# Differential attention's output norm: squares moved from GpSimd to ScalarE, their sum and products placed as steps of their own

## The chip, the cores and the metric

One core of one Trainium2 chip runs the whole program. The metric is the device time of one execution in microseconds; what is compared is the median of several runs. TensorE (PE) does matmuls and transposes, VectorE (DVE), ScalarE (ACT) and GpSimd (POOL) the elementwise work, SyncE (SP) issues the DMAs.

## What is computed

Two layers over x (512 tokens by 1024). Each layer normalizes and modulates x, projects it with w_in (1024 by 3712) and feeds three branches whose outputs are concatenated and go through w_out. Branch A is the one that the change touches most:

```python
def diff_attention(q, k, v, lam, lam_init, subln_g):     # 4 heads, two 32-wide softmax maps each, 64-wide values
    ...
    def block(qi):
        s = jnp.einsum('bqhmd,bkhmd->bhmqk', qi, k).astype(jnp.float32) * scale
        p = jax.nn.softmax(s, axis=-1)
        pd = p[:, :, 0] - lam * p[:, :, 1]
        return jnp.einsum('bhqk,bkhd->bqhd', pd.astype(v.dtype), v)
    ...
    return rms_norm(o, subln_g) * (1.0 - lam_init)
```

After it, A's output is multiplied by its own gate (ga). Branch B is dilated attention with gate gb, branch C bidirectional retention, whose output is normalized over 96 columns of each head and gated by gc.

## The kernel before, in words

The projection is cut into **groups**: one group is six matmuls (L338, L339, L340: the weights split into a high and a low part, whi and wlo, times the high and low part of h) for one tile of 128 tokens and two slices of 128 rows of w_in. whi is rounded on ScalarE from the loaded rows, wlo is their difference on VectorE (L307); both live in a pool of three buffers (tags whi and wlo of `wp`), so that a whi can be written only when the matmuls of the third one before it are done. Everything else hangs on this list: `at(g, fn)` plans a step behind group g, and the program is issued group by group with its planned steps. A scheduler then orders the instructions of each engine, moving ahead what it takes to be ready; `tc.keep_in_program_order` ties an instruction to its place behind all that was issued before it on its engine.

Branch A runs as two units per layer, A0 and A1, B as three, B0 to B2, and they overlap: while A0 ends, B0's scores are running, and while A1 ends, B1's and B2's and branch C's gate. A unit of A (class `Diff`) does its scores (L724), the maximum mx (L726), exp into e on ScalarE, the mix of two maps on VectorE, four transposes through the one transposing PSUM buffer (`tr4`, L555), copies pt, and the pv product (L701). `finish` copies pv to oat; `finish2`, four groups later, transposes oat, copies it to oao (ScalarE), squares it on GpSimd into oasq (L748), sums the squares on VectorE (L752), multiplies twice by r0 (L753, L754) and ends the norm with `rms_end` (L570 on VectorE, a power of -1/2 on GpSimd, L198). `finish3` multiplies by r0 once more (L761), scales oao (L762) and multiplies by ga on GpSimd (L764); `finish4` transposes and splits the result. B's units have scores L785 and L786, a custom maximum L790, a softmax kept in sb (ScalarE) with its reciprocal L796. The scores of A and B, and ada_ps (the sums for the modulation), share two PSUM buffers (`sc_p`). "nat" is q and k after transposing (two writes by ScalarE, two by VectorE, which must be done before the transposing buffer is free), "qkn" their normalized form. Branch C squares its output on ScalarE already (csq), sums on VectorE (css, L962), and multiplies (L968) C_NORM groups after its product; its gate is cth (tanh on ScalarE from the projection's PSUM, then L158 on VectorE), whose buffers the first matmuls of gb (L334) wait for. The gate of the layer's output (ScalarE, gate<-ada_ps) lives in two buffers that ga uses too, so it waits for L764.

Of the kernel before, what the change touches and what calls it, by code (L numbers as in the profile page):

```python
# [9 lines left out]
F32 = mybir.dt.float32  # L10
F32R = mybir.dt.float32r
AF = mybir.ActivationFunctionType
OP = mybir.AluOpType
AX = mybir.AxisListType
# [5 lines left out]
P = 128  # L20
# [20 lines left out]
MODS = 12  # L41
H_0, H_1 = 8, 9
C_GAP, C_DECAY, C_TURN, C_STATE = 3, 4, 4, 7
C_ATT, C_PAIR, C_OUT, C_STEP, C_SUMS, C_NORM = 8, 3, 13, 2, 1, 7
GATE, GATE_GAP, GATE_END = 55, 24, 18
GB_OUT = 9
SETUP, TABLES, RET_T, TAB1 = 12, 12, 19, 9      
N_A1, N_B1, N_SOFT = 5, 5, 9
E_T1, E_T2, E_X, E_QF, E_SCALE_A, E_SCALE_B = 1, 1, 1, 0, 0, 0
FIN2, FIN3, FIN4 = 4, 12, 16  # L50
X_BACK = 2


# [80 lines left out]
def encoder(ctx, tc, x, c, norm_g, w_ada, b_ada, w_in, w_out, params, consts, out):  # L134
# [9 lines left out]
    sm = pool("sm", 4)  # L144
# [6 lines left out]
    V, A, G, T = nc.vector, nc.scalar, nc.gpsimd, nc.tensor  # L151
    dma = nc.sync.dma_start

    def act(o, i, f=AF.Copy, **kw):
        A.activation(o, i, f, **kw)  # L155
# [7 lines left out]
    def at(g, fn, *args):  # L163
        plan.setdefault(g, []).append((fn, args))
# [180 lines left out]
    def tok_(t):  # L345
        return slice(t * P, (t + 1) * P)
# [205 lines left out]
    def tr4(blocks):  # L552
        ps = tr_p.tile([P, 4, P], F32, name="tr")
        for i, b in enumerate(blocks):
            T.transpose(ps[:, i, :], b, ident)  # L555
        return ps
# [12 lines left out]
    def rms_end(s, n, width):  # L569
        V.tensor_scalar(s, s, 1.0 / width, EPS, OP.mult, OP.add)  # L570
        pow_half(s, s, n)
# [132 lines left out]
    class Diff(Attention):  # L704
# [38 lines left out]
        def finish2(self, g):  # L743
            ps = tr4([self.ob[:, tok_(t)] for t in range(NT)])
            o = self.o = ep.tile([P, 8, DV_A], F32, name="oao", tag="e")
            act(o.rearrange("p g d -> p (g d)"), ps.rearrange("p t m -> p (t m)"))
            sq = ep.tile([P, 8, DV_A], F32, name="oasq", tag="e")
            G.tensor_tensor(sq, o, o, OP.mult)  # L748
            ss = self.ss = sm.tile([P, 8], F32, name="oass")
            r0 = self.r0 = sm.tile([P, 8], F32, name="oar0")  # L750
            V.reciprocal(r0.rearrange("p (t h) -> p t h", h=2), self.ssum[:, :, 0::2])
            V.tensor_reduce(ss, sq, AX.X, OP.add)  # L752
            V.tensor_tensor(ss, ss, r0, OP.mult)  # L753
            V.tensor_tensor(ss, ss, r0, OP.mult)  # L754
            rms_end(ss, 8, DV_A)
            at(g + FIN3, self.finish3)
            at(g + FIN4, self.finish4)

        def finish3(self):
            o, ss = self.o, self.ss  # L760
            V.tensor_tensor(ss, ss, self.r0, OP.mult)  # L761
            V.tensor_tensor(o, o, ss.unsqueeze(2).to_broadcast([P, 8, DV_A]), OP.mult)  # L762
            on = o.rearrange("p (t h) d -> p t (h d)", h=2)
            G.tensor_tensor(on, on, self.u.ga, OP.mult)  # L764
# [65 lines left out]
    class Retention:  # L830
# [129 lines left out]
        def sums(self, n):  # L960
            ss = self.ss[n] = sm.tile([P, H_C], F32, name="css")
            tc.keep_in_program_order(V.tensor_reduce(ss, self.sq[n], AX.X, OP.add))  # L962
            rms_end(ss, H_C, DV_C)
# [335 lines left out]
```

## Time and profile before

| | |
|---|---|
| median of 3 runs | 650.28 us (649.83 to 650.92) |
| the profiled execution's own time | 653.0 us |
| its span | 651.2 us, mean granted TensorE clock 0.989 |
| PE, DVE, ACT, POOL busy | 625.5, 496.8, 340.2, 164.4 us |

The rows further down are times from the start of that span. A row of the timeline that has brackets tells how long its engine stood idle in front of it and what ended that. Idle time of TensorE is the only idle time that lengthens this program directly, and a time saved elsewhere counts when it shortens one of those.

### The profile page before, as it was taken

Reading aid. Unit: us, or ns where it says so; the run is one execution under the profiler, and the core shown is the slowest. Engines: PE = TensorE matmul, PEld = TensorE weight load, DVE = VectorE, ACT = ScalarE, POOL = GpSimd, SP = SyncE. Lnnn points to the kernel's source line nnn. Section 1 sums busy time; section 2 is a strip of 40 time slices with the busy share of each in tenths; the row PEclk is TensorE's granted clock in tenths of the full one; section 3 lists DMA queues with packets and bytes.
Section 4 is the critical chain, followed back from the end, with each engine's and each line's share of the span. In section 5 each row is a group of like instructions: output and inputs, shape, how many; then the busy total and the mean of one; then the engine's idle time right before and its main releaser. Section 6 shows DMA issues by size and latency. Waiting matters only on the chain.

```text
span 651.2 us, 10473 instructions
## 1 busy us (share of the span) xinstructions
PE 625.5 (96%) x3487; PEld 514.2 (79%) x3487; DVE 496.8 (76%) x1212; ACT 340.2 (52%) x750; POOL 164.4 (25%) x183
## 2 busy tenths in 40 slices
PE   6999999999999996999999999999999999899997
PEld 1878888987888873677779998997788787677786
DVE  1889776789978986997869374778997996677543
ACT  4744362666746665564434244455756567656410
POOL 1105462514360510200411041632323340010000
PEclk9799999999999998999999999999999999999999
DMA  9987123426565557476643322235555453603211
GB/s 315 334 290 207 40 82 88 133 91 152 147 177 167 125 172 175 141 254 224 185 169 96 90 72 67 77 101 154 142 171 137 142 142 103 163 32 139 89 64 65
DMA packets 87133, 93.03 MB, mean 143 GB/s; under 512 B 7044, under 2 KB 68132, under 8 KB 87080
## 3 DMA queue, kind: packets, MB, share of 16 engines
q1 hardware_dynamic: 87080, 92.37, 47.8%
q8 instruction: 28, 0.46, 0.3%
q14 instruction: 25, 0.20, 0.1%
HBM read 72.42 MB, written 4.19 MB: 118 GB/s over the span
## 4 chain that ended last, share of the span: by engine, by line
PE 77%; DVE 11%; issue 5%; POOL 3%; DMA 2%; ACT 2%; SPq 0%; POOLq 0%; ACTq 0%; DVEq 0%
PE acc L338 15%; PE acc L340 15%; PE acc L339 15%; PE tr L555 8%; PE pv L701 5%; PE sc L724 2%; PE acc L334 2%; PE acc L335 1%; PE acc L336 1%; DVE ada_acc L158 1%; PE sc L785 1%; DVE wlo L307 1%; PE sc L786 1%; PE line L519 1%; PE co L954 1%
## 5 line engine op out<-in xcount | busy, mean ns | idle before, releaser
L338 PE MATMUL acc<-whi,hT 128*128 128x384 f32 (+1 forms) x424 | 155.1, 366 | 0.0
L339 PE MATMUL acc<-wlo,hT 128*128 128x384 f32 (+1 forms) x424 | 152.3, 359 | 0.0
L340 PE MATMUL acc<-whi,hL 128*128 128x384 f32 (+1 forms) x424 | 152.0, 358 | 0.0
L307 DVE TENSOR_TENSOR wlo<-raw,whi 128x384 fp32r<-128x384 f32 (+1 forms) x130 | 81.8, 658 | 27.0 <-ACT whi L155 26.7
L198 POOL TENSOR_TENSOR qkss<-qkss,nhalf 128x4 f32<-128x4 f32 (+1 forms) x40 | 52.6, 1316 | 128.3 <-DVE qkss L570 125.7
L338 PEld LDWEIGHTS acc<-whi,hT 128*128 128x128 f32 x424 | 79.9, 188 | 6.1
L340 PEld LDWEIGHTS acc<-whi,hL 128*128 128x128 f32 x424 | 79.8, 188 | 6.2
L339 PEld LDWEIGHTS acc<-wlo,hT 128*128 128x128 f32 x424 | 79.9, 188 | 5.5
L155 ACT ACTIVATE whi<-raw 128x768 fp32r<-128x768 f32 (+2 forms) x67 | 59.6, 890 | 36.8 <-PE acc L340 34.0
L158 DVE SCALAR_TENSOR_TENSOR ada_acc<-raw,cs,ada_acc 128x512 f32<-128x512 f32 x86 | 64.4, 750 | 7.1 <-DMA raw<-in_w_ada_dram 5.9
L155 ACT ACTIVATE e<-sc,mx 128x512 f32<-128x512 f32 x64 | 43.9, 688 | 35.8 <-DVE mx L726 17.2
L726 DVE TENSOR_REDUCE mx<-sc 128x1 f32<-128x512 f32 x64 | 43.5, 685 | 9.6 <-PE sc L724 9.1
L155 ACT ACTIVATE sb<-sb,mx 128x512 f32<-128x512 f32 x48 | 34.4, 717 | 20.5 <-DVE mx L790 20.2
L701 PE MATMUL pv<-pt,v 128*64 128x256 f32 x320 | 40.1, 394 | 0.6 <-DVE pt L691 0.5
L155 ACT ACTIVATE pt<-tr 128x512 f32<-128x512 f32 x40 | 23.8, 596 | 24.2 <-PE tr L555 24.1
L790 DVE CUSTOM_DVE_ANT_0 sb<-sc,cst 128x512 f32<-128x512 f32 x48 | 32.1, 684 | 5.4 <-PE sc L786 3.5
L555 PE MATMUL tr<-cst,sb 128*128 128x128 f32 x192 | 30.5, 282 | 5.3 <-DVE nat L158 2.2
L701 PEld LDWEIGHTS pv<-pt,v 128*64 128x64 f32 x320 | 21.7, 140 | 16.6 <-DVE pt L691 5.3
L555 PEld LDWEIGHTS tr<-cst,sb 128*128 128x128 f32 x192 | 22.1, 142 | 15.8 <-ACT pt L155 7.3
L691 DVE COPY pt<-tr 128x512 f32<-128x512 f32 x40 | 27.4, 684 | 8.4 <-PE tr L555 8.4
L622 POOL TENSOR_TENSOR qkn<-qkraw,qkss 128x256 f32<-128x256 f32 x40 | 30.4, 760 | 5.8 <-DVE qkraw L618 2.0
L724 PE MATMUL sc<-stk,stq 96*128 96x512 f32 x64 | 27.3, 434 | 0.9 <-ACT e L155 0.9
(293 smaller groups left out, 1368.9 us busy)
## 6 DMA issues: line engine op xcount, KB each, us to landing
raw<-in_w_ada_dram SPq DMA_DIRECT2D x64, 256.0 KB, 4.8
raw<-in_w_in_dram SPq DMA_DIRECT2D x48, 192.0 KB, 2.6
raw<-in_w_in_dram SPq DMA_DIRECT2D x24, 384.0 KB, 3.9
raw<-in_w_in_dram SPq DMA_DIRECT2D x32, 256.0 KB, 3.6
raw<-in_w_ada_dram SPq DMA_DIRECT2D x16, 512.0 KB, 5.4
raw<-in_w_out_dram SPq DMA_DIRECT2D x32, 256.0 KB, 2.8
x<-in_x_dram SPq DMA_DIRECT2D x8, 512.0 KB, 3.5
stB<-nat SPq DMA_DIRECT2D x32, 128.0 KB, 2.3
```

The source lines that it names most:

```text
L155: A.activation(o, i, f, **kw)
L158: V.scalar_tensor_tensor(o, a, s, b, op0, op1)
L198: G.tensor_tensor(o, i, nhalf[:, :n], OP.pow)
L307: V.tensor_tensor(l2[:, z], r2[:, z], h2[:, z].bitcast(F32), OP.subtract)
L338: T.matmul(ps, ah, hi[i], start=s_, stop=False)
L339: T.matmul(ps, ah, lo[i], start=False, stop=False)
L340: T.matmul(ps, al, hi[i], start=False, stop=e_)
L555: T.transpose(ps[:, i, :], b, ident)
L701: T.matmul(self.pv[h * 64:h * 64 + 64, i * 256:i * 256 + 256], self.u.v[:, k, h * 64:h * 64 + 64], self.pt[h][:, k], start=k == 0, stop=k ...
L724: T.matmul(ps, self.u.stq[0:96, m, tok_(qt)], self.u.stk[0:96, m], start=True, stop=True)
L726: V.tensor_reduce(mx, ps, AX.X, OP.max, negate=True)
L790: V.tensor_tensor_reduce(sb, ps, cst[:, m0:m0 + S], 1.0, 3e38, OP.add, OP.min, mx)
```

## The change

The squares go to ScalarE. Their sum, the two products by r0 and `rms_end` become a step `sums` that is planned FIN_S = 2 groups behind `finish2`, with the sum tied to its place; the third product is tied to its place at FIN3 = 12 groups behind. For branch C, sum and product are each planned one group later.

```diff
-C_ATT, C_PAIR, C_OUT, C_STEP, C_SUMS, C_NORM = 8, 3, 13, 2, 1, 7
+C_ATT, C_PAIR, C_OUT, C_STEP, C_SUMS, C_NORM = 8, 3, 13, 2, 2, 8
...
-FIN2, FIN3, FIN4 = 4, 12, 16
+FIN2, FIN_S, FIN3, FIN4 = 4, 2, 12, 16
...
             sq = ep.tile([P, 8, DV_A], F32, name="oasq", tag="e")
-            G.tensor_tensor(sq, o, o, OP.mult)
-            ss = self.ss = sm.tile([P, 8], F32, name="oass")
+            act(sq, o, AF.Square)
             r0 = self.r0 = sm.tile([P, 8], F32, name="oar0")
             V.reciprocal(r0.rearrange("p (t h) -> p t h", h=2), self.ssum[:, :, 0::2])
-            V.tensor_reduce(ss, sq, AX.X, OP.add)
+            at(g + FIN_S, self.sums, sq)
+            at(g + FIN3, self.finish3)
+            at(g + FIN4, self.finish4)
+
+        def sums(self, sq):
+            r0 = self.r0
+            ss = self.ss = sm.tile([P, 8], F32, name="oass")
+            tc.keep_in_program_order(V.tensor_reduce(ss, sq, AX.X, OP.add))
             V.tensor_tensor(ss, ss, r0, OP.mult)
             V.tensor_tensor(ss, ss, r0, OP.mult)
             rms_end(ss, 8, DV_A)
-            at(g + FIN3, self.finish3)
-            at(g + FIN4, self.finish4)
 
         def finish3(self):
             o, ss = self.o, self.ss
-            V.tensor_tensor(ss, ss, self.r0, OP.mult)
+
+            tc.keep_in_program_order(V.tensor_tensor(ss, ss, self.r0, OP.mult))
```

In the changed program the sum is L758, the two products L759 and L760, the third L766, the scaling of oao L767; B's scores L785 and L786 become L790 and L791, and other lines behind it move by five too.

The order of VectorE at the end of A0 in layer 0, as a difference (plus: changed program; names with numbers are one of several buffers; rt, qkraw and qkss belong to the next unit's q and k):

```order
-L691 COPY pt<-tr 128x4x128
-L616 TENSOR_TENSOR rt_2330<-qkraw,ropebs 128x64
-L617 TENSOR_TENSOR rt_2329<-qkraw,ropebc 128x64
-L761 TENSOR_TENSOR oass<-oass,oar_2138 128x8
-L762 TENSOR_TENSOR oao<-oao,oass 128x512
-L307 TENSOR_TENSOR wlo<-raw,whi 128x384 x2
-L608 TENSOR_REDUCE qkss<-qkn 128x4
-L726 TENSOR_REDUCE mx<-sc 128x1
-L570 TENSOR_SCALAR qkss<-qkss 128x4
+L570 TENSOR_SCALAR qkss<-qkss 128x4
+L307 TENSOR_TENSOR wlo<-raw,whi 128x384 x2
+L608 TENSOR_REDUCE qkss<-qkn 128x4
```

The third product L761 and the scaling L762 go from this place (their successors L766 and L767 come some 60 rows further down), so that nothing that waits for GpSimd's power stands in front of the maximum mx. The sum, L758 for L752, stays where it was, eight rows above this piece, and waits for ScalarE in place of GpSimd.

The order of ScalarE in layer 1 where A1 ends, as a difference (nat_6346 and nat_6348 are the two halves that ScalarE writes):

```order
 L155 ACTIVATE nat_6346<-tr,gcol 128x256
-L155 ACTIVATE sb,bs<-sb,mx 128x512
+L155 ACTIVATE sb<-sb,bs 128x512
+L155 ACTIVATE whi<-raw 128x2x384
 L155 ACTIVATE nat_6348<-tr,gcol 128x256
-L155 ACTIVATE sb<-sb,bs 128x512
-L155 ACTIVATE pt<-tr 128x4x128
-L155 ACTIVATE whi<-raw 128x2x384
+L155 ACTIVATE pt<-tr 128x4x128
 L155 ACTIVATE sb,bs<-sb,mx 128x512 x2
```

The rounding of a weight, whi, stood behind both halves of nat and behind a copy pt; now it stands, with a row sb, between the two halves. A few rows further down, at all four ends of a unit, oasq stands right behind oao or one row later, ahead of the e, cth and pt that follow.

TensorE in layer 1 at the same place, first the program before (the rows behind the last B scores up to the next ones):

```order
L338 MATMUL acc<-whi,hT 128x384
L339 MATMUL acc<-wlo,hT 128x384
L340 MATMUL acc<-whi,hL 128x384
L338 MATMUL acc<-whi,hT 128x384
L339 MATMUL acc<-wlo,hT 128x384
L340 MATMUL acc<-whi,hL 128x384
L338 MATMUL acc<-whi,hT 128x384
L555 MATMUL tr<-cst,sb 128x128 x4
L339 MATMUL acc<-wlo,hT 128x384
L340 MATMUL acc<-whi,hL 128x384
L555 MATMUL tr<-cst,sb 128x128 x4
```

and the changed one, from the transposes of qkn on:

```order
L555 MATMUL tr<-cst,qkn 128x128 x4
L338 MATMUL acc<-whi,hT 128x384
L790 MATMUL sc<-stB,stC 128x512
L791 MATMUL sc<-stB,stC 128x512
L339 MATMUL acc<-wlo,hT 128x384
L340 MATMUL acc<-whi,hL 128x384
L338 MATMUL acc<-whi,hT 128x384
L339 MATMUL acc<-wlo,hT 128x384
L340 MATMUL acc<-whi,hL 128x384
L555 MATMUL tr<-cst,sb 128x128 x8
L790 MATMUL sc<-stB,stC 128x512
L791 MATMUL sc<-stB,stC 128x512
```

Between the transposes of qkn and the next of sb there were twelve matmuls of groups, and there are six; of the two matmuls between two fours of transposes of sb none is left, since the groups run further ahead of this chain. The whi of the piece above goes into the buffer whose last readers are these matmuls: it can start when the sixth is done. In layer 0 the same chain loses three matmuls between two such fours. The step gate<-ada_ps moves too: in layer 0 by six rows of ScalarE, in layer 1 by seventeen, behind three roundings of weights and two copies pt, because the ga product in front of it (L764, on GpSimd) comes later.

## Rows read from the trace of the kernel before

**Rows 1.** From the page's parts 1 and 4: busy time and share of the span of each engine with its number of instructions, and the shares of the chain that ended last.

```profile
PE 625.5 (96%) x3487; PEld 514.2 (79%) x3487; DVE 496.8 (76%) x1212; ACT 340.2 (52%) x750; POOL 164.4 (25%) x183
...
PE 77%; DVE 11%; issue 5%; POOL 3%; DMA 2%; ACT 2%; SPq 0%; POOLq 0%; ACTq 0%; DVEq 0%
```

**Rows 2.** Timeline of layer 0, around the end of branch A's first unit, 184 to 211 us, of ScalarE, VectorE and TensorE. Columns: start, duration, engine, line, operation, out<-in, count, and in brackets the idle time before and what ended it.

```profile
184.76 0.60 ACT L155 ACTIVATE pt<-tr 128x512 f32<-128x512 f32 x1
...
185.44 0.62 PE L555 MATMUL tr<-cst,sb 128*128 128x128 f32 x4
...
186.58 0.69 DVE L752 TENSOR_REDUCE oass<-oasq 128x8 f32<-128x512 f32 x1 [1.90 <-POOL oasq L748]
...
189.94 0.17 DVE L761 TENSOR_TENSOR oass<-oass,oar 128x8 f32<-128x8 f32 x1 [0.89 <-POOL oass L198]
...
193.11 0.68 DVE L726 TENSOR_REDUCE mx<-sc 128x1 f32<-128x512 f32 x1
...
194.71 0.50 PE L785 MATMUL sc<-stB,stC 128*128 128x512 f32 x1 [0.94 <-ACT e L155]
...
210.23 0.50 PE L724 MATMUL sc<-stk,stq 96*128 96x512 f32 x1 [0.87 <-ACT e L155]
```

**Rows 3.** The same view at the same place of layer 1, 494 to 509 us.

```profile
494.92 0.21 DVE L616 TENSOR_TENSOR rt<-qkraw,ropebs 128x64 f32<-128x64 f32 x1
...
497.39 0.74 DVE L616 TENSOR_TENSOR rt<-qkraw,ropebs 128x64 f32<-128x64 f32 x1
...
497.01 1.04 POOL L748 TENSOR_TENSOR oasq<-oao 128x512 f32<-128x512 f32 x1
...
498.74 0.61 ACT L155 ACTIVATE pt<-tr 128x512 f32<-128x512 f32 x1
...
499.41 0.65 PE L555 MATMUL tr<-cst,sb 128*128 128x128 f32 x4
...
501.22 0.17 DVE L761 TENSOR_TENSOR oass<-oass,oar 128x8 f32<-128x8 f32 x1 [1.75 <-POOL oass L198]
...
508.25 0.50 PE L785 MATMUL sc<-stB,stC 128*128 128x512 f32 x1 [0.56 <-ACT e L155]
```

**Rows 4.** Timeline of TensorE in layer 1 around the end of A's second unit, 556 to 570 us: transposes, the pv product and gb's first matmul; the column in brackets is its idle time and who ended it.

```profile
556.23 0.60 PE L555 MATMUL tr<-cst,qkn 128*128 128x128 f32 x4
556.59 0.42 PE L339 MATMUL acc<-wlo,hT 128*128 128x384 f32 x1
...
557.30 0.34 PE L340 MATMUL acc<-whi,hL 128*128 128x384 f32 x1
557.48 0.34 PE L338 MATMUL acc<-whi,hT 128*128 128x384 f32 x1
...
559.30 0.63 PE L555 MATMUL tr<-cst,sb 128*128 128x128 f32 x4
...
560.62 0.66 PE L555 MATMUL tr<-cst,sb 128*128 128x128 f32 x4 [0.34 <-ACT pt L155]
...
562.06 1.95 PE L701 MATMUL pv<-pt,v 128*64 128x256 f32 x16 [0.31 <-DVE pt L691]
...
569.03 0.79 PE L334 MATMUL acc<-hT,whi 128*128 128x512 f32 x1 [0.32 <-DVE cth L158]
```

**Rows 5.** The same stretch, ScalarE and VectorE.

```profile
556.87 0.48 ACT L155 ACTIVATE nat<-tr,gcol 128x256 fp32r<-128x256 f32 x1 [1.53 <-PE tr L555]
...
557.95 0.46 ACT L155 ACTIVATE nat<-tr,gcol 128x256 fp32r<-128x256 f32 x1
...
560.46 0.83 ACT L155 ACTIVATE whi<-raw 128x768 fp32r<-128x768 f32 x1
...
558.68 0.48 DVE L158 SCALAR_TENSOR_TENSOR nat<-tr,gcol,nat 128x256 fp32r<-128x256 f32 x1
...
567.41 0.60 ACT L155 ACTIVATE oao<-tr 128x512 f32<-128x512 f32 x1 [2.19 <-PE tr L555]
567.91 0.48 ACT L155 ACTIVATE cth<-acc 128x384 f32<-128x384 f32 x1
...
576.70 0.60 ACT L155 ACTIVATE gate<-ada_ps 128x512 f32<-128x512 f32 x1
```

**Rows 6.** The same place of layer 0: TensorE's idle times, the pv product, and ScalarE's and TensorE's rows around the gate, 249 to 273 us.

```profile
249.53 0.63 PE L555 MATMUL tr<-cst,sb 128*128 128x128 f32 x4 [2.23 <-DVE nat L158]
...
252.37 3.12 PE L701 MATMUL pv<-pt,v 128*64 128x256 f32 x16
...
271.45 0.60 ACT L155 ACTIVATE gate<-ada_ps 128x512 f32<-128x512 f32 x1 [1.50 <-POOL oao L764]
...
272.10 0.50 PE L785 MATMUL sc<-stk,stq 128*128 128x512 f32 x1 [0.63 <-ACT gate L155]
```

**Rows 7.** Granted clock of TensorE by stretch (the windows view: PE, weight load, DVE, ACT and POOL busy with counts, clock, DMA share, GB/s).

```profile
250.00:260.00 10.00, 7.61 (x42) 4.36 (x40) 5.17 (x13) 4.42 (x9) 0.43 (x1) 0.83 0.83 199
570.00:580.00 10.00, 10.00 (x52) 7.58 (x52) 7.72 (x22) 5.45 (x12) 3.16 (x2) 0.89 0.00 0
```

**Rows 8.** Tile view of branch C's squares: each operation with its minimum, median and maximum in ns; below, who waited for it.

```profile
L155 ACT ACTIVATE csq<-cno x8: 513/525/526, 110.7 to 431.0; 128x384 f32<-128x384 f32 x8
  DVE css L962: 10.2, 6
```

## What the change does to the time, predicted before it ran

> **What bounds the kernel now.** I read the page first, then TensorE's timeline from end to end for every place where it stands idle, then the other engines' timelines at those places. TensorE is busy for 625.5 of 651.2 us [rows 1], so the whole program has 25.7 us in which it waits, and a change that leaves its work alone can move the time only through that remainder. The chain that ended last agrees: 77% TensorE, 11% VectorE, 2% ScalarE, 3% GpSimd [rows 1]. GpSimd's squares, which the change takes away, are therefore worth nothing by their own duration; the question is which TensorE waits lie behind them, and which new ones come.
>
> Two kinds of places matter. Where a unit A0 ends, groups of projection matmuls are plentiful and TensorE hardly waits: 0.94 us at 194.71 and 0.87 us at 210.23 in layer 0 [rows 2], 0.56 us at 508.25 in layer 1 [rows 3]. Where A1 ends, the groups have run out, and TensorE follows a chain of transposes, copies on ScalarE and VectorE, and further transposes: 2.23 us before one transpose in layer 0 [rows 6], 0.34, 0.31 and 0.32 us before three instructions in layer 1 [rows 4]. There each half microsecond that a link of the chain gains or loses goes straight into the time, and each group matmul that was already spent is missing as cover.
>
> **The change part by part.**
>
> *Squares off GpSimd, A0.* VectorE's sum waited 1.90 us for GpSimd's squares and the third product 0.89 us for its power; the score maximum behind them began at 193.11, and the exp, hence TensorE's scores, came late by 0.94 us [rows 2]. In layer 1 the product alone waited 1.75 us, and TensorE 0.56 us after it [rows 3]. In the changed order the third product is no longer in front of that maximum, and the sum waits for ScalarE. Both TensorE waits are shorter than the VectorE waits in front of them, so I count both as gone: 0.94 + 0.56 = 1.50 us. The 0.87 us at 210.23 stand after a copy and an exp on ScalarE that the change does not touch: counted as unchanged, 0.87 us for the low end.
>
> *Squares on ScalarE.* No row has this instruction. Branch C's squares of 384 columns take 0.525 us [rows 8]; a ScalarE copy of 512 columns takes 0.60 us and the next one starts 0.50 us after it (567.41 to 567.91) [rows 5]. So what stands behind is put back by 0.40 us (the squares, less the 0.10 us of overlap) to 0.60 us; I take 0.50, the row of the same width. At A0 that falls on pt: it was ready 0.08 us before its transposes began in layer 0 (184.76 + 0.60 against 185.44) [rows 2] and 0.06 us in layer 1 (498.74 + 0.61 against 499.41) [rows 3], so TensorE would wait 0.42 and 0.44 us, if no more matmuls come between; the change has them in other places, so I take 0 and 0.86 us as bounds and 0.34 us for both together, nearer to the middle since one more matmul (0.18 us, 557.30 to 557.48 [rows 4]) covers part.
>
> *cth behind the squares, A1.* At both ends of A1 the squares stand between oao and cth. gb's first matmul already waited 0.32 us for cth in layer 1 [rows 4], so nothing covers the shift: 0.50 us each, 1.00 us. Bounds 0.80 and 1.20 us by those of the instruction.
>
> *Groups that ran ahead, A1.* In layer 0 three matmuls are missing between transposes, 0.53 us. In layer 1 two are missing where TensorE waits 0.34 us for pt already [rows 4], 0.35 us. Together 0.88 us; the low bound is 0, where the chain itself comes that much earlier.
>
> *The rounding whi between the halves of nat, layer 1.* This is the largest term. Count from the start of the qkn transposes (556.23) [rows 4]. The first half of nat starts 0.64 us later (556.87) [rows 5]. The six matmuls that are left, and the two score matmuls, are through at about 1.95 us, and the last one's end, 2.11 us, is what whi waits for. ScalarE runs whi for 0.83 us and overlaps the next by 0.10 us [rows 5], so the second half of nat starts at about 2.85 us where it started at 1.72 (557.95) [rows 5]. From there to the next transposes the trace has 1.35 us (557.95 to 559.30) [rows 4, 5], of which 0.27 us are a VectorE row in front of its half (558.41 to 558.68). The transposes thus start between 3.93 and 4.20 us, and TensorE has been idle since 1.95: 1.98 to 2.25 us of new wait. The single transposing buffer lets nothing pass. I take 1.90 us, since the clock of these rows can differ by a little; the low bound is 0, if whi's buffer comes free before or the chain runs ahead.
>
> *Moved for nothing.* The gate in layer 0 cost TensorE 0.63 us, because it waited 1.50 us for GpSimd's ga product with a score buffer held [rows 6]. It now stands further down; that 0.63 us goes, but the two score pairs behind it share one PSUM buffer and each waits for VectorE's reading (0.68 us for a row of that width [rows 2]). I set these against each other: 0, with −0.63 and +0.8 us as bounds. In layer 1 the gate was at 576.70 without a wait of TensorE [rows 5]; its delay is the same risk, +0.8 us. Branch C's sum waited 10.2 us for its squares [rows 8], all on VectorE while TensorE had groups; one group later takes these waits away and shortens nothing. SP and its DMAs change places by single rows; loads are far ahead.
>
> Here GpSimd's share of the memory interfaces is to be weighed. While its squares run (497.01 to 498.05), a VectorE product with two inputs takes 0.74 us, where the same one takes 0.21 us else [rows 3]. So one of the four squares cost VectorE 0.53 us. The Trainium skill (GPSIMD Engine Reference, section Key points) says that GpSimd shares its SBUF interfaces with VectorE and contends with VectorE instructions of two SBUF inputs; the trace agrees at this place. By that rule the sum would have up to 0.53 us less, if VectorE were what TensorE waits for there. The row's place is the one whose TensorE wait is counted as gone already, so I add nothing.
>
> **The sum**: −1.50 + 0.34 + 1.00 + 0.88 + 1.90 = +2.62 us. It is made against the profiled execution (653.0 us, span 651.2); the median of the three runs is 650.28, 2.7 us below, and the difference is put on the median: 652.9 us.
>
> **The rivals.** What a measurement tells from no change is about 0.2%, 1.3 us: faster is below 649.0, slower above 651.6.
>
> *Faster.* The order of the chain at A1 is written for a TensorE that is later than it will be, and VectorE sets the pace. If the 2.79 and 1.75 us that VectorE no longer waits bring the chain forward, the waits of 0.94, 0.87, 0.56 and 0.63 us all go (3.0 us), the group matmuls that ran ahead were covered, and only the two cth cost 1.00 us: 648.3 us. For it: all four lie behind GpSimd or VectorE. Against: at the end of A1 TensorE's waits name pt and cth, and GpSimd stands behind none of them [rows 4]. It decides if the second half of nat in layer 1 is ready before the six matmuls are done.
>
> *No change.* All terms hold but the wait behind whi, because whi's buffer is free earlier or ScalarE takes nat's second half in time: +2.62 − 1.90 = +0.72, 651.0 us. For it: 0.72 is what is left of many small terms of both signs.
>
> *Slower by more.* TensorE's granted clock was 0.83 of full in the ten us after the 2.23 us wait of layer 0, and 0.89 from 570 us in layer 1 [rows 7]; the pv product of sixteen matmuls took 3.12 us in the first [rows 6] and 1.95 in the second [rows 4], so half the clock costs it 1.17 us. If the new wait in layer 1 puts pv at the lower level too, and the gate's buffer costs 0.8 us, it is 652.9 + 1.17 + 0.8 = 654.9 us.
>
> **How the numbers follow.** Forecast (slower by the wait behind whi) 0.42; slower by more 0.11; no change 0.25; faster 0.22. The likeliest is the forecast, 652.9 us; its own range, from 0.7 less of the whi wait and of the chain to 0.8 more for the gate, is 651.6 to 654.0. Signs of both kinds hold weight, so the range reaches to the faster case and past the slower: 648.1 to 655.1 us.
>
> **What would show it.** Right: in the changed trace ScalarE's cth starts about 1.0 us after oao in place of 0.5, at both ends of A1; the scores at the two A0 places start without 0.94 and 0.56 us; in layer 1 the transposes of sb behind those of qkn stand 1.5 to 2.3 us behind nat; the gate of layer 1 starts ten us or more after 576.70. Wrong: no wait above 0.5 us at those transposes (then 651.0 or less), or TensorE's idle total below 23 us in place of 25.7 (then faster); a longer stretch below full clock with the same waits would be the slower rival.

## The result, and the profile after

The changed kernel takes 656.06 us (median of 20 runs, 651.3 to 658.03), the kernel before 651.92 us on the same chip (20 runs, 649.08 to 655.4). The ratio is 1.0058, 95% interval 1.0040 to 1.0076: slower by 3.8 us (the two medians lie 4.1 us apart). The forecast's sum was +2.62 us, a ratio of 1.0040; the time itself lies 1 us above the range, for two reasons of unequal kind: the loss is 1.2 us larger than the sum, and the three runs that the sum was put on (650.28 us) lie 1.6 us below the twenty. Three executions far above all others (694.59 us of e1, 2127.04 us of e11, 3431.2 us of the kernel before, beside e5 to e8) are left out of every ratio.

The profiled execution of the changed kernel took 656.07 us. From its page, the parts shown of before in [rows 1]: span, busy time, chain that ended last.

```profile
span 654.3 us, 10490 instructions
...
PE 627.6 (96%) x3487; PEld 516.9 (79%) x3487; DVE 491.1 (75%) x1212; ACT 341.8 (52%) x754; POOL 157.4 (24%) x179
...
PE 89%; DVE 7%; ACT 2%; issue 1%; DMA 1%; SPq 0%; POOL 0%; DVEq 0%
```

The span grew by 3.1 us (651.2 to 654.3). TensorE does the same 3487 instructions and is busy 2.1 us longer, with a granted clock whose mean fell from 0.989 to 0.984. Its idle time grew by only 1.0 us, but that is a balance: 4.1 us of its waits are gone, and 5.5 us are new or longer. Gone are 0.94, 0.87 and 0.63 us in layer 0 [rows 2, 6] and 0.56 us in layer 1 [rows 3], and two more that the prediction did not name (0.57 us in front of transposes at 162 us, 0.54 us in front of a matmul at 322 us). New, or longer, are these. TensorE's timeline in both layers, idle time in brackets:

```profile
261.12 0.79 PE L334 MATMUL acc<-hT,whi 128*128 128x512 f32 x1 [0.97 <-DVE cth L158]
...
537.03 1.95 PE L701 MATMUL pv<-pt,v 128*64 128x256 f32 x16 [1.18 <-DVE pt L691]
...
557.48 0.60 PE L555 MATMUL tr<-cst,qkn 128*128 128x128 f32 x4
...
559.31 0.34 PE L340 MATMUL acc<-whi,hL 128*128 128x384 f32 x1
...
561.67 0.63 PE L555 MATMUL tr<-cst,sb 128*128 128x128 f32 x4 [2.02 <-DVE nat L158]
...
562.98 0.65 PE L555 MATMUL tr<-cst,sb 128*128 128x128 f32 x4 [0.69 <-ACT pt L155]
...
572.06 0.80 PE L334 MATMUL acc<-hT,whi 128*128 128x512 f32 x1 [0.97 <-DVE cth L158]
```

ScalarE in layer 1, the counterpart of [rows 5]:

```profile
558.74 0.45 ACT L155 ACTIVATE nat<-tr,gcol 128x256 fp32r<-128x256 f32 x1
559.10 0.71 ACT L155 ACTIVATE sb<-sb,bs 128x512 f32<-128x512 f32 x1
559.71 0.82 ACT L155 ACTIVATE whi<-raw 128x768 fp32r<-128x768 f32 x1
560.44 0.46 ACT L155 ACTIVATE nat<-tr,gcol 128x256 fp32r<-128x256 f32 x1
...
569.78 0.60 ACT L155 ACTIVATE oao<-tr 128x512 f32<-128x512 f32 x1 [2.19 <-PE tr L555]
570.41 0.63 ACT L155 ACTIVATE oasq<-oao 128x512 f32<-128x512 f32 x1
570.95 0.85 ACT L155 ACTIVATE cth<-acc 128x384 f32<-128x384 f32 x2
...
593.00 0.60 ACT L155 ACTIVATE gate<-ada_ps 128x512 f32<-128x512 f32 x1 [0.81 <-POOL oao L769]
```

Both chains of the forecast can be followed. whi stands between the halves of nat; the second half starts at 560.44, 1.70 us after the first, and TensorE, whose last group matmul began at 559.31, waits 2.02 us. The squares stand between oao and cth: cth starts 1.17 us after oao where it was 0.50, and gb's first matmul waits 0.97 us where it was 0.32 us [rows 4].

The 1.18 us at 537.03 are a new place. VectorE and GpSimd in front of it, same timeline:

```profile
533.91 1.27 DVE L570 TENSOR_SCALAR qkss<-qkss 128x4 f32<-128x4 f32 x1
...
536.30 0.68 DVE L691 COPY pt<-tr 128x512 f32<-128x512 f32 x1
...
533.87 1.28 POOL L769 TENSOR_TENSOR oao<-oao,ga 128x512 f32<-128x512 f32 x1
```

A VectorE operation on four columns takes 1.27 us where its median is 0.16 us, and it ends (535.18) within 0.03 us of GpSimd's ga product (535.15), which the later third product has brought beside it. The copy pt, which pv waits for, stands a few operations behind it on VectorE. The place is new, but the effect is not: the trace of before has it on the same line of code in layer 0.

```profile
219.28 0.61 DVE L570 TENSOR_SCALAR qkss<-qkss 128x4 f32<-128x4 f32 x1
...
220.54 0.16 DVE L570 TENSOR_SCALAR qkss<-qkss 128x4 f32<-128x4 f32 x1
...
219.25 0.61 POOL L622 TENSOR_TENSOR qkn<-qkraw,qkss 128x256 f32<-128x256 f32 x1
219.82 1.06 POOL L198 TENSOR_TENSOR qkss<-qkss,nhalf 128x4 f32<-128x4 f32 x1
```

Beside GpSimd's product of 256 columns (L622) the operation takes 0.61 us and ends with it; beside GpSimd's power of four columns (L198) it takes 0.16 us. The Trainium skill (GPSIMD Engine Reference, section Key points) says that GpSimd shares its SBUF interfaces with VectorE, and that there is contention with VectorE instructions that have two SBUF inputs or run in a 2-port performance mode. This operation has one input; whether it runs in such a mode no run here shows.

The granted clock, in the windows view (PE, weight load, DVE, ACT, POOL busy with counts, clock, DMA share, GB/s):

```profile
40.00:60.00 20.00, 18.39 (x92) 15.82 (x91) 16.95 (x41) 7.68 (x13) 10.10 (x20) 0.83 0.87 244
...
260.00:275.00 15.00, 14.03 (x69) 10.32 (x68) 12.49 (x33) 7.70 (x18) 2.16 (x2) 0.89 0.41 133
555.00:580.00 25.00, 19.31 (x111) 13.70 (x110) 13.87 (x37) 12.95 (x27) 1.64 (x1) 0.93 0.40 106
```

and the second of these windows in before:

```profile
260.00:275.00 15.00, 13.97 (x73) 9.86 (x72) 14.02 (x35) 8.08 (x18) 4.34 (x4) 1.00 0.46 160
```

After the 0.97 us at 261.12 the stretch to 275 us has 0.89, where before has 1.00; from 555 us both have 0.93. The stretch from 40 us, far from any edit, has 0.83. Two more profiles of the same changed kernel (e4 and e10) have 0.89 again from 260 us, but 1.00 from 40 us and 0.86 from 555 us: some of the stretches that fall to the lower level (1.2 GHz in place of 2.4) differ from one execution of a kernel to the next. So one profile cannot price the clock, and the experiments below compare means over runs.

### The profile page after: what moved, and what is told of

It reads as the page before. It is cut to its first block, busy times and chain, and to the rows that moved or that the text cites. A ratio compares the mean times of both kernels' runs of the same rounds, so it can differ in the third digit from the quotient of the medians.

```text
span 654.3 us, 10490 instructions
## 1 busy us (share of the span) xinstructions
PE 627.6 (96%) x3487; PEld 516.9 (79%) x3487; DVE 491.1 (75%) x1212; ACT 341.8 (52%) x754; POOL 157.4 (24%) x179
## 3 DMA queue, kind: packets, MB, share of 16 engines
HBM read 72.42 MB, written 4.19 MB: 117 GB/s over the span
## 4 chain that ended last, share of the span: by engine, by line
PE 89%; DVE 7%; ACT 2%; issue 1%; DMA 1%; SPq 0%; POOL 0%; DVEq 0%
PE acc L340 18%; PE acc L338 18%; PE acc L339 17%; PE tr L555 10%; PE pv L701 6%; PE sc L724 3%; PE acc L334 2%; PE acc L335 2%; PE acc L336 2%; PE sc L790 2%; PE sc L791 2%; PE line L519 1%; PE co L959 1%; DVE ada_acc L158 1%; PE kv L926 1%; PE co L958 1%
## 5 line engine op out<-in xcount | busy, mean ns | idle before, releaser
L307 DVE TENSOR_TENSOR wlo<-raw,whi 128x384 fp32r<-128x384 f32 (+1 forms) x130 | 78.6, 634 | 35.0 <-ACT whi L155 34.7
L198 POOL TENSOR_TENSOR qkss<-qkss,nhalf 128x4 f32<-128x4 f32 (+1 forms) x40 | 55.7, 1393 | 133.6 <-DVE qkss L570 93.8
L622 POOL TENSOR_TENSOR qkn<-qkraw,qkss 128x256 f32<-128x256 f32 x40 | 28.5, 712 | 7.7 <-DVE qkraw L618 2.0
```

The costliest lines, as they stand in the source:

```text
L198: G.tensor_tensor(o, i, nhalf[:, :n], OP.pow)
L307: V.tensor_tensor(l2[:, z], r2[:, z], h2[:, z].bitcast(F32), OP.subtract)
```

## The experiments

**Theories.** T1, that of the forecast: TensorE's waits set the time, made of cth behind the squares, the wait behind whi, and the waits at A0. T2: the waits are only a part, and the granted clock that goes with them is most of the loss. T3, which came up later: what makes the neighbourhood fragile is that cth is taken from the ring of five buffers (tag "e" of `ep`) that oao, oasq, oat, sb and e share; with a buffer of its own gb's matmuls need not stand behind that chain.

Two columns below are worked out from the runs. "Waits" is the sum of TensorE's waits of 0.05 us or more in the profiled execution (before 21.67, change 22.85 us). One of these waits, for the constants' load at the start, lies between 4.16 and 5.22 us without any edit that touches it (before 4.17, change 4.26, e1 5.22, e2 4.75, e3 4.16, e4 4.89, e6 4.55 us), so differences of less than 1 us in this column need it taken off. "Full clock" is an estimate: over all runs together, time fits a constant of the kernel plus some 533 us times (1 − mean granted clock) within 0.6 us rms, and the constant is the time that the kernel would have at clock 1.0. Ratios are to the kernel before on the same chip, with 95% intervals. e1 to e4 share a chip, and so do e5 to e8, e9 to e12 and e13 to e15; from one of these groups to another the ratios are the safer comparison. e1 to e8 have twelve runs each, e9 and e12 four, e11 and e13 to e15 six.

| run | median us | ratio | waits us | mean clock | full clock us |
|---|---|---|---|---|---|
| before | 651.92 | 1 | 21.67 | 0.990 to 0.991 | 647.05 |
| the change | 656.06 | 1.0058 (1.0040 to 1.0076) | 22.85 | 0.984 | 647.15 |
| e1 C only | 653.76 | 1.0010 (0.9988 to 1.0032) | 22.03 | 0.987 | 646.4 |
| e2 A only | 655.27 | 1.0039 (1.0020 to 1.0058) | 21.22 | 0.983 | 646.0 |
| e3 A only, squares late | 650.54 | 0.9976 (0.9955 to 0.9996) | 20.19 | 0.989 | 644.7 |
| e4 the change again | 656.94 | 1.0049 (1.0023 to 1.0075) | 23.42 | 0.983 | 647.2 |
| e5 the change, squares late | 653.35 | 1.0022 (1.0002 to 1.0042) | 21.97 | 0.987 | 646.3 |
| e6 engine of the squares only | 655.13 | 1.0041 (1.0024 to 1.0057) | 22.11 | 0.984 | 646.1 |
| e7 A only, A1's squares on GpSimd | 652.56 | 1.0013 (0.9993 to 1.0034) | 21.02 | 0.988 | 645.9 |
| e8 as e3, without the ties | 650.61 | 0.9969 (0.9950 to 0.9988) | 20.46 | 0.990 | 644.65 |
| e9 before, cth's own buffer | 638.71 | 0.9808 (0.9786 to 0.9830) | 13.62 | 0.996 | 636.9 |
| e11 the change, cth's own buffer | 633.88 | 0.9730 (0.9710 to 0.9750) | 11.39 | 0.997 | 632.4 |
| e12 as e8, cth's own buffer | 639.16 | 0.9804 (0.9781 to 0.9828) | 13.87 | 0.996 | 636.2 |
| e13 A only, cth's own buffer | 638.18 | 0.9788 (0.9762 to 0.9815) | 12.37 | 0.995 | 635.1 |
| e14 C only, cth's own buffer | 637.24 | 0.9776 (0.9752 to 0.9801) | 12.59 | 0.996 | 635.1 |
| e15 as e6, cth's own buffer | 639.12 | 0.9801 (0.9775 to 0.9827) | 12.88 | 0.996 | 636.4 |

**e1, C's part alone.** Only the table line of the diff.

```diff
-C_ATT, C_PAIR, C_OUT, C_STEP, C_SUMS, C_NORM = 8, 3, 13, 2, 1, 7
+C_ATT, C_PAIR, C_OUT, C_STEP, C_SUMS, C_NORM = 8, 3, 13, 2, 2, 8
```

> Branch C's sum and product one group later, branch A as before. Theory (the new TensorE wait comes from the order around whi): in this order too the rounding whi stands between the two halves of nat in layer 1, so TensorE waits 2.0 us before the transposes of sb there and 0.69 in place of 0.34 before the next ones; A0's waits of 0.94, 0.87 and 0.56 us remain, cth waits stay at 0.31 and 0.32. TensorE's idle total 24 us in place of 21.7; time +2.4 us (ratio 1.004), up to +3.6 if the clock drops there too. Rival (C's step is hidden, the wait comes from A's part): idle total 21.7, ratio 1.000.

TensorE's timeline of this kernel in layer 1:

```profile
558.02 0.33 PE L340 MATMUL acc<-whi,hL 128*128 128x384 f32 x1
...
560.36 0.63 PE L555 MATMUL tr<-cst,sb 128*128 128x128 f32 x4 [2.01 <-DVE nat L158]
```

The wait behind whi comes with C's one-group delay by itself, without any edit of branch A. Against the expectation, 0.94 and 0.87 us of layer 0's A0 are gone in it too, and the time does not change measurably (+0.1%, interval across 1). So the largest term of the sum belonged to the part that the prediction had listed under "moved for nothing".

**e2, A's part alone**: the diff without that line.

```diff
-C_ATT, C_PAIR, C_OUT, C_STEP, C_SUMS, C_NORM = 8, 3, 13, 2, 2, 8
+C_ATT, C_PAIR, C_OUT, C_STEP, C_SUMS, C_NORM = 8, 3, 13, 2, 1, 7
```

> Branch A's change alone, C's constants as before. Theory: no whi between the halves of nat, so no 2.02 us wait; A0's waits of 0.94, 0.87 and 0.56 us and the gate's 0.63 are gone, cth waits 0.97 twice; idle total 19.5 to 21 us, time 0.5 to 2 us below before (ratio 0.997 to 0.999) and 2.5 to 4 us below the whole change. Rival (squares on ScalarE cost what the change costs): ratio 1.004 or more, idle total above 22.

No wait of 2.0 us, as expected; yet 1.0039 where 0.997 to 0.999 was expected. Its waits are 0.45 us less than before's (1.03 us less without the wait at the start), but its clock is as low as that of the whole change. The 0.87 us of A0 are still there, so it is C's line that removes them, and gb waits 0.97 us for cth in layer 0 and 0.52 us in layer 1. VectorE and TensorE of this kernel:

```profile
533.46 0.69 DVE L691 COPY pt<-tr 128x512 f32<-128x512 f32 x1
534.06 1.16 DVE L570 TENSOR_SCALAR qkss<-qkss 128x4 f32<-128x4 f32 x1
...
261.25 0.52 PE L334 MATMUL acc<-hT,whi 128*128 128x512 f32 x1 [0.97 <-DVE cth L158]
```

Here VectorE's small operation is stretched beside the ga product too (1.16 us), but stands behind the copy pt, and no pv waits. The 1.18 us of the whole change thus take both parts: A's moves the product there, C's puts the copy behind the operation.

**e3, A's part with the squares two groups later**, behind cth instead of ahead of it; **e5**, the same in the whole change.

```diff
         def finish2(self, g):
...
-            sq = ep.tile([P, 8, DV_A], F32, name="oasq", tag="e")
-            act(sq, o, AF.Square)
...
-            at(g + FIN_S, self.sums, sq)
+            at(g + FIN_S, self.sums)
...
-        def sums(self, sq):
-            r0 = self.r0
+        def sums(self):
+            r0, o = self.r0, self.o
+            sq = ep.tile([P, 8, DV_A], F32, name="oasq", tag="e")
+            act(sq, o, AF.Square)
```

> As the one with A's change alone, but the squares are issued two groups later with the sum, so that cth goes ahead of them on ScalarE. Theory: cth's waits fall from 0.97 to 0.31 at both places, idle total 1.3 us less than with A's change alone; time 1 to 2 us less than that, 1.5 to 4 us below before (ratio 0.994 to 0.998). Rival (the matmuls behind cth are covered by other work, or the delay returns at pt): waits move to the transposes behind, time as with A's change alone.

> The whole change, C's part included, but with the squares issued with the sum, behind cth. Theory (the squares in front of cth make the loss: TensorE stands longer in front of gb's first matmul and then runs a stretch at the lower clock): cth waits 0.31 twice, the 2.0 us wait of layer 1 remains, idle total 21.3 to 22; clock 0.986 to 0.989; ratio 0.998 to 1.002, 3 to 4 us below the whole change. Rival (the 2.0 us wait behind whi makes the loss, as the prediction had it): ratio stays at 1.004 or more.

e3 is faster than before (0.9976). It is 4.7 us faster than e2 by the medians and 4.1 us by the ratios, where 1 to 2 us were expected, and the two differ in nothing but where these four squares are issued and take their buffer. Its timeline of ScalarE and TensorE, layer 0:

```profile
258.73 0.60 ACT L155 ACTIVATE oao<-tr 128x512 f32<-128x512 f32 x1 [2.19 <-PE tr L555]
259.22 0.48 ACT L155 ACTIVATE cth<-acc 128x384 f32<-128x384 f32 x1
259.59 0.63 ACT L155 ACTIVATE oasq<-oao 128x512 f32<-128x512 f32 x1
...
260.35 0.50 PE L334 MATMUL acc<-hT,whi 128*128 128x512 f32 x1 [0.31 <-DVE cth L158]
```

and the windows of e2 and e3 at the same place:

```profile
260.00:275.00 15.00, 14.03 (x69) 10.22 (x68) 12.25 (x31) 7.80 (x18) 2.16 (x2) 0.89 0.31 107
```

```profile
260.00:275.00 15.00, 14.69 (x80) 10.86 (x80) 14.40 (x38) 8.26 (x19) 3.33 (x3) 1.00 0.39 134
```

The first is e2, the second e3: 69 matmuls at 0.89 against 80 at 1.00. The waits account for little of it: 21.22 to 20.19 us, of which 0.59 us are the wait at the start. By the fit the clock, 0.983 to 0.989, accounts for some 3.1 us (0.0059 times 533 us), and 1.3 us remain at full clock. e5 is better than the whole change in the same way, by 1.8 us on e4's ratio (1.0049 to 1.0022; 3.6 us by the medians, which are from two chips) where 3 to 4 us were expected. It keeps the 2.02 and the 1.19 us, and stays slower than before.

**e4 and e10, the whole change again**, unedited: 656.94 us (twelve runs) and 656.56 us (one run, clock 0.981).

> The whole change once more, beside the parts on one chip. Idle total 22.9 us, ratio 1.004 to 1.0076. If the clock and not the waits makes most of the difference, its granted clock is lower than that of the parts whose waits are as long; if the waits make it, C's step alone and A's step alone add up to it: ratio of C alone times ratio of A alone equals this one within 0.002.

This test does not decide. The ratios of C alone and A alone multiply to 1.0010 times 1.0039 = 1.0049, which is e4's ratio and was the sign for the waits; but each of the three ratios is uncertain by the 0.002 that was to tell, and the clock's losses could add up just as well. The sign for the clock cannot be read, since neither part has waits as long as e4's.

**e6, only the engine of the squares**, everything else as before; **e7**, A's part with A1's squares left on GpSimd.

```diff
-            G.tensor_tensor(sq, o, o, OP.mult)
+            act(sq, o, AF.Square)
```

```diff
-            act(sq, o, AF.Square)
+            if self.k == 0:
+                act(sq, o, AF.Square)
+            else:
+                G.tensor_tensor(sq, o, o, OP.mult)
...
-            Diff(un, g, gap, *out_pair(u))
+            Diff(un, g, gap, *out_pair(u)).k = u
```

> The kernel before with nothing but the squares on ScalarE: no step of its own, nothing tied to its place. Theory: cth waits 0.97 (or 0.9 and 0.5) in place of 0.31, the clock is at half right behind 260 us, mean clock 0.984 or less, ratio 1.002 to 1.006. Rival (the moved sum and the tied products make the loss): ratio 1.000 or below, clock 0.990.

> A's change alone with the squares on ScalarE at A0 and on GpSimd at A1. Theory: no squares in front of cth, so cth waits 0.31 twice, no half clock behind 260 us, clock 0.988 to 0.990, ratio 0.996 to 0.999, like the one with late squares. Rival (ScalarE's squares harm at A0 as well, or the tied products do): ratio 1.002 or more.

TensorE's timeline of e6 at the two A1 ends:

```profile
261.90 0.50 PE L334 MATMUL acc<-hT,whi 128*128 128x512 f32 x1 [1.19 <-DVE cth L158]
...
572.03 0.50 PE L334 MATMUL acc<-hT,whi 128*128 128x512 f32 x1 [1.19 <-DVE cth L158]
```

e6 carries most of the loss in one line: gb waits 1.19 us for cth at both A1 ends, clock 0.984, ratio 1.0041. Without the wait at the start the sum of its waits is that of before (17.56 against 17.50 us), since the 0.94 and 0.56 us of A0 and the gate's 0.63 us are gone in it; what it loses is the clock. e7, where cth waits cost 0.31 us as before, is at 1.0013 with the clock at 0.988. So most of the loss comes from the squares at A1. That those at A0 cost nothing is not shown: e7 missed its expected 0.996 to 0.999, and it is slower than e3 (0.9976), with intervals that hardly touch.

**e8, e3 without `tc.keep_in_program_order`** at the sum and the third product.

```diff
-            tc.keep_in_program_order(V.tensor_reduce(ss, sq, AX.X, OP.add))
+            V.tensor_reduce(ss, sq, AX.X, OP.add)
...
-            tc.keep_in_program_order(V.tensor_tensor(ss, ss, self.r0, OP.mult))
+            V.tensor_tensor(ss, ss, self.r0, OP.mult)
```

> A's change with late squares, nothing tied to its place. In its order the third product stands right behind the sum again, in front of the score maximum, and waits for GpSimd's power there. Theory (tying the third product gives the gain at A0): the waits of about 0.9 us at 195 and 0.5 us at 508 are back, idle total 1.0 to 1.8 us above the one with late squares and ties, ratio 0.998 to 1.001. Rival (late squares alone give the gain): the same as with ties within 0.1%.

650.61 us, the same as e3, so its rival holds: the waits of 0.94 and 0.56 us did not return without the ties. e6 lacks them too, with no tie and no step of its own, so the squares' engine alone is enough to remove them.

**e9 and e11 to e15, cth in a buffer of its own**, in before, in the whole change, and in the kernels of e8, e2, e1 and e6.

```diff
-            th = ep.tile([P, 384], F32, name="cth", tag="e")
+            th = one.tile([P, 384], F32, name="cth")
```

> The kernel before with one edit: cth has a buffer of its own instead of one of the five that e, sb, oat, oao and oasq share. Theory (A1's end is slow because cth waits for one of those five, and gb's matmuls wait for cth): cth moves up on ScalarE by some ten instructions, gb's matmuls stand between the transposes; the waits between 250 and 261 us and between 560 and 570 us (2.7 and 2.7 us without the first ones for nat) shrink to under 1 us each; idle total 16 to 18 us in place of 21.7; no half clock behind 560 us; ratio 0.985 to 0.994. Rival (the chain of transposes and copies itself is the limit): waits move, idle total over 20 us, ratio above 0.997.

> The whole change with a buffer of its own for cth, so that the squares no longer stand in front of it. Theory (the loss of the change is its delay of cth): the change turns from a loss of 0.5% into no loss against the kernel before with the same edit: ratios of the two within 0.003, and both below 0.995. Rival (the loss is in the moved sums, the tied products or C's step): it stays 3 us or more behind the kernel before with that edit.

> A's change without ties, squares late, cth in a buffer of its own; C as before. The version that the runs so far point to. Theory: idle total 15 to 18 us, ratio 0.982 to 0.992, 1 to 3 us below the kernel before with its own cth buffer. Rival: no better than that one.

> A's change alone, C as before, cth in a buffer of its own. If A's squares and ties make the 4 to 5 us between the kernel before and the whole change (both with that buffer), ratio 0.972 to 0.976 and A0's waits of 0.95 and 0.56 us gone; if C's step makes them, ratio 0.979 to 0.983, like the kernel before with that buffer.

> C's sum and product one group later, A as before, cth in a buffer of its own. If A's part makes the gain, ratio 0.979 to 0.983; if C's step does, 0.973 to 0.977. With cth out of the way the whi between the halves of nat should cost less, because gb's matmuls can run in that time: no TensorE wait over 0.6 us in front of those transposes, where it was 2.0 us.

> The kernel before with the squares on ScalarE and cth in a buffer of its own. This edit cost 0.4% with the shared buffers (cth 1.19 us late twice, clock 0.984). Theory: with its own buffer cth is done before the squares begin, and the same edit costs nothing: ratio 0.977 to 0.982, clock 0.995 or more. Rival (squares on ScalarE cost by themselves): ratio 0.984 or more.

Before becomes 13.2 us faster, more than was expected, the change some 22 us faster than it was, and the order turns: the change is now the fastest of all, by 4.8 us against e9 (633.88 to 638.71), where at best no loss was expected. And e15 is level with e9 (0.9801 and 0.9808): with this buffer the squares on ScalarE cost nothing. ScalarE and TensorE of e11 in layer 1:

```profile
545.34 0.49 ACT L155 ACTIVATE cth<-acc 128x384 f32<-128x384 f32 x1 [0.66 <-DVE cno L980]
...
557.40 0.60 ACT L155 ACTIVATE oao<-tr 128x512 f32<-128x512 f32 x1 [1.26 <-PE tr L555]
558.03 0.63 ACT L155 ACTIVATE oasq<-oao 128x512 f32<-128x512 f32 x1
...
545.05 0.60 PE L555 MATMUL tr<-cst,qkn 128*128 128x128 f32 x4
...
546.85 0.39 PE L334 MATMUL acc<-hT,whi 128*128 128x512 f32 x1
...
548.72 0.60 PE L555 MATMUL tr<-cst,sb 128*128 128x128 f32 x4
```

and its windows view over the stretch that had three long waits:

```profile
540.00:565.00 25.00, 25.00 (x150) 19.27 (x149) 19.82 (x57) 18.09 (x39) 1.85 (x1) 1.00 0.48 127
```

The first cth starts 12 us ahead of oao and not behind it; gb's matmuls begin between the transposes of qkn and sb, and cover them. TensorE is busy for all 25 us, at 1.00. In the other kernels with this buffer A's part and C's part gain 1.8 us each at full clock (e13 and e14 against e9: 636.9 to 635.1), and both together 4.5 us (to 632.4). The two single gains are not clear of noise (the ratios 0.9788 and 0.9776 have intervals that overlap with e9's 0.9808), and neither part makes the whole gain alone. e12 missed its expectation: it is no better than e9. Part of what sets e11 apart is seen in the traces: in e12 and e15 TensorE waits 1.85 and 1.84 us for the gate in layer 1, and in e14 1.60 us for a copy pt, where e11 waits 0.31 us for that gate. The 1.18 us at pv remain in e11, at 524.43, with the stretched operation (1.27 us) in front.

## Why the prediction was off

The forecast was a sum of TensorE's waits. The step that failed is the granted clock, which that sum put at nothing: it makes 2.1 of the 3.1 us between the two profiles, and nearly all of the loss by the fit over the runs. Besides, one new wait was not foreseen, and the base was 1.6 us too low.

- **Direction and mechanisms at A1 held.** cth: taken as 0.50 us at each end, measured 0.66 and 0.65 (0.31 to 0.97, 0.32 to 0.97), since the squares take 0.63 us and cth starts 1.17 us behind oao. Behind whi: 1.90 taken, 2.02 measured; from the start of the qkn transposes (557.48) nat's second half starts 2.96 us later where the count had 2.85, and the transposes of sb 4.19 us later where it had 3.93 to 4.20. Groups that ran ahead: 0.88 taken; 0.35 us came in layer 1 (0.34 to 0.69) and 0.60 in layer 0. These three sum to 4.28 where the sum had 3.78. The gate of layer 1 starts 16 us later, as forecast, and TensorE does not wait for it.
- **The gains were larger.** 1.50 was counted and came; so did the 0.87 us at 210.23 that was counted as unchanged, and the gate's 0.63 us without the 0.8 us set against it, and 0.57 and 0.54 us elsewhere: 2.61 us more. The 0.34 us for pt behind the squares did not come.
- **The wait that was not foreseen.** The prediction weighed what GpSimd's work does to VectorE at the place where the squares went away, and added nothing. It did not ask where GpSimd's ga product, moved by the same edit, goes to: beside another VectorE operation that stands in front of a copy that TensorE waits for, 1.18 us. The trace of before had shown that operation stretched (0.61 us at 219.28).
- **The step on C.** "Shortens nothing" was read from C's own waits (10.2 us of VectorE, now 1.7, indeed worth nothing on TensorE). As a table entry it changes the order of everything behind it: e1 has the 2.0 us and the cleared A0 waits in layer 0, all from that line.
- **The clock was left out of the sum.** It stood only in the rival "slower by more", with a chance of 0.11, and there for one pv product. Waits alone come to +1.2 us in the two profiles (4.28 + 1.18 − 4.11, and small ones), less than half of the sum's 2.62, so that the measured 3.8 us lie near the sum is luck. The rest is the clock: 2.1 us of busy time in the two profiles, and 3.7 us by the fit over the runs (0.991 to 0.984), which leaves 0.1 us at full clock. The two ways of counting differ by more than 1 us, so the clock's share is known only as between two thirds and nearly all. e2 against e3 and e6 against e7 show the same: the kernels in which gb waits longer for cth (the change, e2, e4, e6) have 0.983 or 0.984, those where it waits 0.31 or 0.32 us (before, e1, e3, e5, e7, e8) have 0.987 to 0.991. It is not that wait alone: the profile of e5 has 0.89 from 260 to 275 us after a cth wait of 0.31 us. How the chip comes to that from these waits was not tested, and stays open.
- **The base.** A median of three was used as if it were exact; twenty runs put the kernel before 1.6 us higher. On that base the sum gives 654.5 us, and the range would have ended at 656.7. (The narrower range of the likeliest case does not follow from its words: 0.8 us more than 652.9 is 653.7, not 654.0.)

## What to carry to other kernels

Price a delay by who waits for the delayed step's buffer and how much filler stands behind that wait: the four squares cost over 4 us when they stand ahead of one small tanh and not behind it (e2 against e3), and giving that tanh its own buffer was worth 13 us. Where an edit has several parts and a scheduler orders the program, measure the parts alone, since a one-number change can own the largest wait. Count the granted clock as a term of its own where an edit makes TensorE wait longer between matmuls (here its share was the larger one), and follow where work of GpSimd lands, not only where it leaves.

## What the runs showed of the hardware

- A VectorE operation on 128x4 numbers with one input was stretched from 0.16 to 1.27 us and ended with GpSimd's 128x512 product beside it. All nine profiles here that bring the two together show it (the change, e2 to e5, e7, e10, e11, e13: 1.16 to 1.27 us); it took 0.18 us in e8, where they are apart. Beside a GpSimd product of 256 columns it took 0.61 us, beside GpSimd's power of four columns 0.16 us (before, 219.28 and 220.54).
- ScalarE's squares of 128x512 take 0.63 us, against 1.04 us for the product on GpSimd [rows 3].
- Two orders of one program whose TensorE waits differ by 1.0 us (0.4 us without the wait at the start) differed by 4.7 us in time (e2, e3), with a mean granted clock of 0.983 against 0.989. e6 and before, with the same sum of waits without that at the start, differed by 0.41% (0.984 against 0.991).
